# One decoder trunk on one core: four more weight chunks of the conditioning are summed during the first MLP, and the stage between the MLPs is issued in another order

## The chip, the cores and the metric

The kernel runs on one core of one Trainium2 chip. The metric is the device time of one execution in microseconds (us). TensorE (PE) multiplies, with its weight loads (PEld) beside it; VectorE (DVE), ScalarE (ACT) and GpSimd (POOL) do the rest; SyncE (SP) issues nearly all loads from HBM through one queue, in order. Engines wait for each other through semaphores.

## The reference

```python
for layer in range(2):                       # D_MODEL 1024, SEQ 256, BATCH 1, float32
    mod = (silu(c) @ ada_w[layer] + ada_b[layer])[:, None, :]
    sh_a, sc_a, gt_a, sh_m, sc_m, gt_m = jnp.split(mod, 6, axis=-1)
    h = modulate(rms_norm(x, attn_norm[layer]), sh_a, sc_a)
    mix = diff_attention(h, ...) if layer == 0 else nsa_attention(h, ..., *shared)
    x = x + gt_a * mix
    h = modulate(rms_norm(x, mlp_norm[layer]), sh_m, sc_m)
    x = x + gt_m * squared_relu_mlp(h, mlp_w1[layer], mlp_w2[layer])   # hidden width 4096
    if layer == 0:
        sh_kv, sc_kv = jnp.split(silu(c) @ kv_ada_w + kv_ada_b, 2, axis=-1)
        shared = nsa_shared_kv(modulate(rms_norm(x, kv_norm), sh_kv, sc_kv), ...)
return rms_norm(x, final_norm)
```

`modulate(h, shift, scale)` is `h * (1 + scale) + shift`. `nsa_attention` has 16 query heads that read one compressed and two full sets of keys and values.

## The kernel before

**Products.** Every weight is brought in as a chunk of 1 MB (`raw`), split by ACT into a rounded high part (`wh`, line 260) and by DVE into the remainder (`wl`, line 262), in two halves each, and multiplied in three products (lines 267 to 269; the rows of `rows_acc` and `proj_t` have these lines). Three chunks can wait as `raw` (pool `rawp`), three as `wh`/`wl` (pool `wp`). A load is issued when the chunk that held its buffer has been split.

**Adaptive weights.** The vectors `mod` come from 48 further chunks of 1 MB, twelve vectors of four chunks each, in a list: `gate(l, 2)` and `gate(l, 5)` are the two gates, `shift` and `scale` the others. A *tick* takes the next chunk and adds it on DVE, in two instructions, to `acc` (lines 416 and 418). After a vector's fourth tick PE turns it (line 447) and DVE finishes it (lines 455 to 458), or, for a gate, PE sums it (line 481) and DVE adds it to `gt` (line 482). Chunks of ticks come from two buffers, and during the first MLP from three more (`lend`).

**Stages.** Layer A's attention; MLP 0; a short stage with the residual (`ORDER_AB`); layer B (`ORDER_B`); MLP 1; the end. An MLP has 16 steps; in a step PE multiplies a chunk of w1 (`proj_t`) and one of w2 (`rows_acc`), ACT applies relu and square (lines 591 and 592), and `ticks[f]` says how many ticks step f has. The stages between are recorded in an order written out by hand as a list of names, each of which advances one generator by a step: `kc`, `vc`, `k1`, `k2`, `g`, `q0` to `q3` are projections, `p` the products of the compressed keys (line 1227), `h0` to `h7` the heads, `r0` to `r2` the output projection, `W` and `w` split steps, `a` a tick, `d` the end of a vector, `F` a load of `cmp_w1`, `x` filler products, `n0` and `n1` the residual and norm of either half of the rows, `y0` and `y1` the first products of MLP 1. `in_order` keeps that order on PE, ACT, DVE and SP.

**Compressed keys.** `kc` and `vc` are projections whose results are copied (`u`, line 1189; for `kc` on DVE, for `vc` on ACT) and rearranged by eight DMAs that POOL issues (`Z`, lines 1192 and 1193); DVE adds positions (`M`, line 1214, steps `m0` and `m1`), and `p` multiplies M with the `cmp_w1` chunks. Queries are scaled from PSUM by ACT (`qs`, line 1262) before the scores (line 1373) and the compressed scores (line 1327).

Of the kernel before, what the change touches and what calls it, by code (L numbers as in the profile page):

```python
# [44 lines left out]
n0 n1 n0 n1 w n0 n1 w v2 x v1 v2 v2 n1 n1 n1 n1 n1 v1 v2 F v1  # L45
"""
ORDER_B = """
kc kc W w W W w W vc a kc a w w W w vc W vc W a W w w k1 F k1 w m0 m1 p p W k1 a k2 W g W p p w W p k2 w g v1 p p p q0
k2 w W q0 w g W z q0 g g q1 h0 w g w W h0 z h0 h1 q1 h0 W h0 h0 q1 h0 h1 z c0 h0 c0 h2 h1 h0 c0 h1 c0 v2 d c0 h0 c0 h0
h2 h1 h2 h1 h0 h1 a h1 h1 h2 h3 h3 h3 q2 w h0 q2 h1 a h1 h3 q2 h2 h2 w h4 h2 W h2 h2 a h3 h2 W q3 w q3 h1 h3 h1 W h4 a  # L50
h2 h5 h3 h3 h3 h5 h4 h5 h4 q3 h5 h2 h3 W h4 w c1 h4 W c1 h3 h5 h4 c1 h6 h5 c1 d h4 d w h4 c1 r0 h4 c1 w h6 w h4 h3 h4
h5 h6 h2 h3 h7 W h5 h4 h6 h5 w h5 h7 r0 h7 r0 h7 h6 h6 h5 h7 r0 h6 h5 h6 r0 a r1 W h6 h7 a W h6 r1 h6 h6 r1 r1 w h5 h6
r1 a h7 h7 h7 w a h7 W h7 h7 h7 r2 w r2 d n0 W r2 n0 w n0 n0 n0 d r2 n0 n1 n0 n0 n1 r2 n1 n0 x n0 n1 x n0 n0 n1 n1 n0
W x n1 n1 y0 y0 n1 n1 n1 n1 w W n1 y0 x w y1 n1 n1 y0 y1 W y1 W w y1 w
"""
ORDER_END = """
r r r r r n0 n0 n0 n0 n0 n1 n1 n0 n1 n1 n1 n1 n1
# [621 lines left out]
def tall(w, i):  # L679
    return [P, 8, 256], [(lambda t: t, w[D * i : D * i + D, :].rearrange("(t p) c -> p t c", p=P))]  # L680
# [38 lines left out]
def trunk(net, scratch):  # L719
# [81 lines left out]
    def ada_steps(key, kind, w, col, finish):  # L801
        items.extend(rows(w[:, col : col + D], 256 * i) for i in range(4))
        net.steps.extend((kind, i, finish) for i in range(4))
# [4 lines left out]
    gate = lambda l, i: ada_steps((l, i), long, ada[l], D * i, net.ada_gate((l, i), ap["ada_b"][l : l + 1, D * i : D * i + D]))  # L808
# [7 lines left out]
    scale(("kv", 1), ap["kv_ada_w"], D, long, kvb[:, 8:16], kvn)  # L816
    shift((1, 0), ada[1], 0, long, adab(1, 0))
    scale((1, 1), ada[1], D, long, adab(1, 1), an(1))
    gate(1, 2)
    shift((1, 3), ada[1], 3 * D, long, adab(1, 3))  # L820
    scale((1, 4), ada[1], 4 * D, long, adab(1, 4), mn(1))
    gate(1, 5)
    weights.steps = weights.high_parts(), weights.low_parts()
    net.ada = Stream(net, net.adap, items, 2)
# [7 lines left out]
    with tc.tile_pool(name="attn_a", bufs=2) as net.work, ExitStack() as slices:  # L832
# [4 lines left out]
        hT = net.pair()  # L837
# [249 lines left out]
        def first_values():  # L1087
            plan.need("v7")
            for g in range(2):
                vv[g] = new("v")  # L1090
                for t in range(2):
                    nc.scalar.copy(vv[g][:, t, :], vs[t][:, g * 256 : g * 256 + 256])
                plan.mark(f"first{g}")
                yield

        def more_bias():
            plan.need("table")
            for g in range(4):
                if g > 1:
                    plan.need(f"scored{g - 2}")  # L1100
                biases[g] = load_bias(net.work, 4 * g, 4, 1)
                yield

        def rows_chunk(i):
            plan.need(f"heads{i}", *(f"rows{j}" for j in range(i)))
            if i == 0:
                acc.extend(net.accumulators())
            steps = weights.until_done(net.rows_acc(acc, [(weights.pop(f"r{i}"), oT, 2 * i)], i == 0, False), 5)
            yield from plan.finally_mark(steps, 5, f"rows{i}")

        def rows_end():
            plan.need("heads2", "heads3", "rows0", "rows1")
            parts = [(weights.pop("r2"), oT, 2 * i) for i in (2, 3)]
            yield from net.last_rows(net.rows_acc(acc, parts, False, True), plan, "sum")

        acc, early_ps, hT2 = [], {}, net.pair_late()
        weights.turns = deque("q2 k2 v2 q3 k3 v3 r0 r1 r2 r2 y0 y1".split())
        plan.work = dict(
            W=weights.steps[0], w=weights.steps[1], a=net.ticks(), d=net.endings(), L=weights.further(), x=net.busy(3), v=first_values(), b=more_bias(),
            r0=rows_chunk(0), r1=rows_chunk(1), r2=rows_end(),  # L1120
            n0=net.token_input(0, acc, lambda: net.mod[(0, 2)], [mods(0, 3)], hT2, plan, "sum"),
            n1=net.token_input(1, acc, lambda: net.mod[(0, 2)], [mods(0, 3)], hT2, plan, "sum"),
# [13 lines left out]
    nc.gpsimd.dma_start(w2c, ap["cmp_w2"].rearrange("s (k p) d -> p s k d", p=P))  # L1136
    spare = ExitStack()
    extra = spare.enter_context(tc.tile_pool(name="spare", bufs=3, side="right"))
    net.ada.lend(extra, 3, 20)
    talls = Stream(net, extra, [tall(ap["cmp_w1"][s], a) for a in range(2) for s in range(2)], 0)  # L1140

    def tall_loads():
# [3 lines left out]

    loads = tall_loads()
    with tc.tile_pool(name="mlp0", bufs=2) as net.work:
        acc, last = net.mlp(hT, early_ps, [0, 0, 4, 1, 1, 2, 1, 1, 2, 1, 1, 2, 2, 2, 0, 0])
        plan = Plan()  # L1150
        pairs = net.pair_late(2)
        given = acc, lambda: net.mod[(0, 5)], [mods("kv", 0), mods(1, 0)], pairs, plan, "sum"
        plan.work = dict(
            W=weights.steps[0], w=weights.steps[1], a=net.ticks(), d=net.endings(), L=weights.further(), F=loads, x=net.busy(3), r=net.last_rows(last, plan, "sum"),
            n0=net.token_input(0, *given), n1=net.token_input(1, *given),
        )
        kv_ps = {}
        weights.turns = deque(["v1", "v2"])
        plan.work.update({f"v{i}": net.early_proj_x(f"v{i}", pairs, plan, 0, kv_ps) for i in (1, 2)})
        plan.run(ORDER_AB)  # L1160
        hkv, hT = pairs

    with ExitStack() as st:
        pool = lambda name, bufs: st.enter_context(tc.tile_pool(name=name, bufs=bufs))
        keep = pool("attn_b1", 1)
        k1 = lambda name, shape: keep.tile(shape, F32, name=name)
# [19 lines left out]
        def for_blocks(s):  # L1186
            ps = yield from project("kv"[s] + "c")
            kvc = net.u([P, 2, T])
            (nc.scalar.copy if s else nc.vector.tensor_copy)(kvc, ps)
            for g in range(2):  # L1190
                src = kvc[g * 64 : g * 64 + 64]
                nc.gpsimd.dma_start(Zv[0:64, s, :, g, :], src)
                nc.gpsimd.dma_start(Zv[64:128, s, :, g, 0:255], src[:, :, 1:256])
            plan.mark(f"pairs{s}")
            yield

        def keys(br):
            ps = yield from project(f"k{br + 1}")
            nc.scalar.copy(kt[:, :, br, :], ps)
            plan.mark(f"keys{br}")  # L1200
            yield

        def values(br):
            nc.scalar.copy(vv[:, br], kv_ps[f"v{br + 1}"])
            plan.mark(f"values{br}")
            yield

        def blocks(s):
            plan.need(f"pairs{s}")
            for a in range(2):  # L1210
                src = Z[:, s].rearrange("p g (n t w) -> p t g n w", w=2, t=8)[:, :, :, a : a + 15, 0]
                dst = M[s][:, 8 * a : 8 * a + 8, 0:60].rearrange("p t (g n) -> p t g n", g=4)
                pb = pos[:, s, 8 * a : 8 * a + 8].unsqueeze(2).unsqueeze(3).broadcast_to([P, 8, 4, 15])
                nc.vector.tensor_add(dst, src, pb)
            plan.mark(f"blocks{s}")
            yield

        z = []
# [81 lines left out]
        def gating():  # L1300
            gps = yield from project("g", act=hT, cols=1, backward=True)
            graw = net.u([P, T])
            nc.scalar.copy(graw, gps[:, 0, :])
            yield
            ps = net.bank([P, 2, P])
            for qb in range(2):
                nc.tensor.transpose(ps[:, qb, :], graw[:, P - qb * P : T - qb * P], ident)
            yield
            nc.vector.tensor_scalar_max(gates, ps[:, :, 80:128], -80.0)
            yield  # L1310
            nc.scalar.activation(gates, gates, AF.Exp, scale=-1.0)
            yield
            nc.vector.tensor_scalar_add(gates, gates, 1.0)
            nc.vector.reciprocal(gates, gates)
            plan.mark("gates")
            yield
# [117 lines left out]
        def rows_end():  # L1434
# [5 lines left out]
        acc, early_ps, pairs, heads_out = [], {}, net.pair_late(), net.pair_late()  # L1440
# [3 lines left out]
            W=weights.steps[0], w=weights.steps[1], a=net.ticks(), d=net.endings(), L=weights.further(), F=loads, x=net.busy(3), kc=for_blocks(0), vc=for_blocks(1),  # L1444
            k1=keys(0), v1=values(0), k2=keys(1), v2=values(1), m0=blocks(0), m1=blocks(1),
            p=block_products(), z=hidden(), g=gating(), c0=compressed(0), c1=compressed(1),
            r0=rows_chunk(0), r1=rows_chunk(1), r2=rows_end(), n0=net.token_input(0, *given), n1=net.token_input(1, *given),
# [7 lines left out]
    with tc.tile_pool(name="mlp1", bufs=2) as net.work:  # L1455
        acc, last = net.mlp(hT, early_ps, [0, 0, 0, 1, 0, 1, 0, 1, 0, 1, 0, 0, 0, 0, 0, 0])
# [19 lines left out]
```

## Time and profile before

| what | us |
|---|---|
| median of 3 runs (716.26 to 718.22) | 716.46 |
| the profiled execution | 716.31 |
| its span, first to last instruction | 714.5 |
| PE busy in it | 676.0 (95%) |
| DVE busy | 533.0 (75%) |
| ACT busy | 390.0 (55%) |

The span is 1.8 us shorter than the execution's own time. In the span, MLP 0 runs from about 175 to 336 us, the residual stage to about 369, layer B to about 515 and MLP 1 from about 528 to 695. A busy share is an average over all stages; which engine the others wait for is read stage by stage.

### The profile page before, as it was taken

To read this page: it belongs to the slowest core of one execution; us is meant where nothing else is said; L and a number is where in the kernel's file an instruction comes from. 1 tells how busy PE (TensorE), PEld (TensorE's weight loads), DVE (VectorE), ACT (ScalarE), POOL (GpSimd) and SP (SyncE) were. 2 spreads that over 40 slices of the span, in tenths; PEclk is the share of its full clock that TensorE was granted. 3 is DMA by queue.
4 is the path that set the end of the run, shared out by engine and by line. 5 is a ranking of instruction groups with operands and counts; after the bars stand their busy time and mean duration, and the time that the engine had idled before them with its cause. 6 is when DMAs were issued, how large, how long until landed. Compare 5 with 4: busy or idle time off the path is not lost.

```text
span 714.5 us, 12065 instructions
## 1 busy us (share of the span) xinstructions
PE 676.0 (95%) x4719; PEld 594.7 (83%) x4719; DVE 533.0 (75%) x1012; ACT 390.0 (55%) x773; POOL 24.5 (3%) x46
## 2 busy tenths in 40 slices
PE   5699999999999999999897999989999999999995
PEld 4588998679889999998796786767799999989984
DVE  5686999888778787786897489889885465564545
ACT  3324976757256455454662268786574545444543
POOL 4010000000000000000002010000000000000000
PEclk9799999999999999999899899989999999999999
DMA  9999887896979888899569962963856557646411
GB/s 276 315 321 339 263 314 282 304 330 201 336 257 320 306 311 291 317 360 314 197 207 273 286 148 92 252 186 122 294 167 216 192 183 274 214 149 201 153 80 59
DMA packets 107272, 173.33 MB, mean 243 GB/s; under 512 B 3568, under 2 KB 78560, under 8 KB 107216
## 3 DMA queue, kind: packets, MB, share of 16 engines
q1 hardware_dynamic: 103840, 163.13, 69.3%
q0 software_dynamic: 2784, 8.38, 4.1%
q10 hardware_dynamic: 592, 1.05, 0.4%
q8 instruction: 37, 0.61, 0.4%
q14 instruction: 19, 0.16, 0.1%
HBM read 170.43 MB, written 1.07 MB: 240 GB/s over the span
## 4 chain that ended last, share of the span: by engine, by line
PE 78%; DMA 9%; DVE 6%; ACT 5%; issue 2%; SPq 0%; ACTq 0%; DVEq 0%
PE ps L267 21%; PE ps L269 20%; PE ps L268 20%; DMA ada_s<-ada_w 3%; DMA raw<-ada_w 2%; ACT e L660 2%; DMA raw<-b_w_out 2%; PE ps L281 2%; PE ps L286 2%; PE ps L282 2%; PE ps L1227 1%; DMA raw<-a_w_in 1%; DVE wl L262 1%; PE ps L1373 1%; PE ps L447 1%
## 5 line engine op out<-in xcount | busy, mean ns | idle before, releaser
L262 DVE TENSOR_TENSOR wl<-raw,wh 128x1024 fp32r<-128x1024 f32 x178 | 209.1, 1214 | 55.5 <-ACT wh L260 55.5
L260 ACT ACTIVATE wh<-raw 128x1024 fp32r<-128x1024 f32 (+1 forms) x178 | 179.1, 1047 | 111.8 <-DMA raw<-mlp_w 43.2
L267 PE MATMUL ps<-ah,wh 128*128 128x256 f32 x648 | 184.3, 284 | 0.0
L269 PE MATMUL ps<-ah,wl 128*128 128x256 f32 x648 | 183.2, 283 | 0.0
L268 PE MATMUL ps<-al,wh 128*128 128x256 f32 x648 | 183.1, 283 | 0.0
L267 PEld LDWEIGHTS ps<-ah,wh 128*128 128x128 f32 x648 | 123.9, 191 | 2.5 <-issue 2.2
L268 PEld LDWEIGHTS ps<-al,wh 128*128 128x128 f32 x648 | 123.9, 191 | 0.0
L269 PEld LDWEIGHTS ps<-ah,wl 128*128 128x128 f32 x648 | 123.8, 191 | 0.0
L267 PE MATMUL ps<-wh,uh 128*128 128x512 f32 (+1 forms) x320 | 113.0, 353 | 0.6 <-ACT uh L598 0.6
L269 PE MATMUL ps<-wh,ul 128*128 128x512 f32 (+1 forms) x320 | 112.1, 350 | 0.0
L268 PE MATMUL ps<-wl,uh 128*128 128x512 f32 (+1 forms) x320 | 111.6, 349 | 0.0
L418 DVE SCALAR_TENSOR_TENSOR acc<-raw,cact,acc 128x1024 f32<-128x1024 f32 x77 | 98.8, 1283 | 4.1 <-DMA raw<-ada_w 2.2
L599 DVE TENSOR_TENSOR ul<-uu,uh 128x512 fp32r<-128x512 f32 x28 | 19.3, 690 | 66.4 <-ACT uh L598 66.4
L267 PEld LDWEIGHTS ps<-wh,uh 128*128 128x128 f32 x320 | 60.3, 188 | 10.1 <-ACT uh L598 1.4
L269 PEld LDWEIGHTS ps<-wh,ul 128*128 128x128 f32 x320 | 60.1, 188 | 9.3 <-DVE ul L599 0.9
L268 PEld LDWEIGHTS ps<-wl,uh 128*128 128x128 f32 x320 | 60.3, 188 | 8.9 <-issue 0.5
L591 ACT ACTIVATE r<-ps 128x512 f32<-128x512 f32 x32 | 19.1, 597 | 86.0 <-PE ps L269 81.5
L660 ACT ACTIVATE e<-e,t 128x128 f32<-128x128 f32 (+1 forms) x96 | 42.4, 448 | 7.3 <-DVE t L655 7.2
L267 PE MATMUL ps<-wh,ah 128*128 128x512 f32 (+1 forms) x128 | 45.6, 357 | 0.0
L268 PE MATMUL ps<-wl,ah 128*128 128x512 f32 (+1 forms) x128 | 43.2, 338 | 0.0
L269 PE MATMUL ps<-wh,al 128*128 128x512 f32 (+1 forms) x128 | 43.2, 337 | 0.0
L655 DVE CUSTOM_DVE_ANT_0 e<-ps,bias 128x128 f32<-128x128 f32 (+1 forms) x96 | 28.3, 353 | 2.6 <-PE ps L667 1.7
(252 smaller groups left out, 965.9 us busy)
## 6 DMA issues: line engine op xcount, KB each, us to landing
raw<-mlp_w SPq DMA_DIRECT2D x64, 1024.0 KB, 8.1
raw<-ada_w SPq DMA_DIRECT2D x40, 1024.0 KB, 6.5
ada_s<-ada_w SPq DMA_DIRECT2D x16, 512.0 KB, 7.8
raw<-kv_ada_w SPq DMA_DIRECT2D x8, 1024.0 KB, 7.8
w_s<-a_w_in SPq DMA_DIRECT2D x8, 768.0 KB, 7.6
raw<-a_w_in SPq DMA_DIRECT2D x6, 1024.0 KB, 5.6
raw<-w_kv SPq DMA_DIRECT2D x6, 1024.0 KB, 7.1
raw<-b_w_in SPq DMA_DIRECT2D x9, 512.0 KB, 9.0
```

The source lines that it names most:

```text
L260: nc.scalar.activation(to(h), of, AF.Copy)
L262: nc.vector.tensor_sub(to(l), of, to(h).bitcast(F32))
L267: mm(out, lh, rh, start=first, stop=False, **kw)
L268: mm(out, lh, rl, start=False, stop=False, **kw)
L269: mm(out, ll, rh, start=False, stop=last, **kw)
L281: mm(ps[:, t, :], hh[:, k, c], wh[:, k, :], start=k == 0, stop=False)
L282: mm(ps[:, t, :], hh[:, k, c], wl[:, k, :], start=False, stop=False)
L418: nc.vector.scalar_tensor_tensor(acc, raw[:, j, :], cc, acc, op0=ALU.mult, op1=ALU.add)
L591: nc.scalar.activation(r, ps, AF.Relu)
L599: nc.vector.tensor_sub(ul, u, uh.bitcast(F32))
L655: self.nc.vector.tensor_tensor_reduce(out=out, in0=s, in1=bias[:, T - n : T], scale=-1.0, scalar=BIG, op0=ALU.add, op1=ALU.min, accum_out=neg)
L660: self.nc.scalar.activation(part, part, AF.Exp, bias=neg, scale=-1.0, accum_out=total)
```

## The change

The list of vectors gets another order at one place: the gate of layer B's attention, `gate(1, 2)`, moves behind the shift and scale of layer B's MLP. MLP 0 has 24 ticks where it had 20, two in each step from 2 to 13, and `ORDER_B` has 8 where it had 12; MLP 1 keeps its 4. The chunks that MLP 0 sums in addition are those of `shift((1, 3))`. `ORDER_B` is a new arrangement of the same steps, less four `a` and two `d`. The arithmetic stays as it was.

```diff
 ORDER_B = """
-kc kc W w W W w W vc a kc a w w W w vc W vc W a W w w k1 F k1 w m0 m1 p p W k1 a k2 W g W p p w W p k2 w g v1 p p p q0
...
+W kc W W kc W w v1 W w vc W kc a vc w w a k1 k1 vc m0 w W w W W k2 m1 w F w a p p W a w k2 g W W p p k2 w k1 g p g d W
...
     scale((1, 1), ada[1], D, long, adab(1, 1), an(1))
-    gate(1, 2)
     shift((1, 3), ada[1], 3 * D, long, adab(1, 3))
     scale((1, 4), ada[1], 4 * D, long, adab(1, 4), mn(1))
+    gate(1, 2)
     gate(1, 5)
...
-    net.ada.lend(extra, 3, 20)
+    net.ada.lend(extra, 3, 24)
...
-        acc, last = net.mlp(hT, early_ps, [0, 0, 4, 1, 1, 2, 1, 1, 2, 1, 1, 2, 2, 2, 0, 0])
+        acc, last = net.mlp(hT, early_ps, [0, 0, 2, 2, 2, 2, 2, 2, 2, 2, 2, 2, 2, 2, 0, 0])
```

**Place 1, DVE at the start of layer B.** Twelve rows up to M0 before, ten up to M1 now. `u ... <-ps` is the copy of `kc`'s result; raw_..._3914 before and raw_..._3945 after is the chunk of `k1`, 4090 and 4096 that of `k2`, 4096 and 4128 that of `g`. Before:

```order
L262 TENSOR_TENSOR wl_593_4093<-raw_582_3914,wh_592_4092 128x1024
L416 TENSOR_SCALAR acc_597_4126<-raw_508_3449,cact_122 128x1024
L418 SCALAR_TENSOR_TENSOR acc_597_4126<-raw_508_3449,cact_122,acc_597_4126 128x1024
L1189 COPY u_599_4131<-ps_588_4036 128x512
L418 SCALAR_TENSOR_TENSOR acc_597_4126<-raw_509_3453,cact_122,acc_597_4126 128x1024 x2
L262 TENSOR_TENSOR wl_593_4093<-raw_582_3914,wh_592_4092 128x1024
L262 TENSOR_TENSOR wl_602_4144<-raw_591_4090,wh_601_4143 128x1024
L418 SCALAR_TENSOR_TENSOR acc_597_4126<-raw_598_4129,cact_122,acc_597_4126 128x1024 x2
L262 TENSOR_TENSOR wl_606_4182<-raw_594_4096,wh_605_4181 128x512
L262 TENSOR_TENSOR wl_602_4144<-raw_591_4090,wh_601_4143 128x1024
L262 TENSOR_TENSOR wl_606_4182<-raw_594_4096,wh_605_4181 128x512
L1214 TENSOR_TENSOR M0_4028<-Z_4027,colB_134 128x8x60 x2
```

Now:

```order
L262 TENSOR_TENSOR wl_604_4131<-raw_599_4096,wh_603_4130 128x1024
L1189 COPY u_607_4163<-ps_598_4070 128x512
L416 TENSOR_SCALAR acc_608_4169<-raw_516_3481,cact_122 128x1024
L418 SCALAR_TENSOR_TENSOR acc_608_4169<-raw_516_3481,cact_122,acc_608_4169 128x1024
L262 TENSOR_TENSOR wl_601_4099<-raw_590_3945,wh_600_4098 128x1024
L418 SCALAR_TENSOR_TENSOR acc_608_4169<-raw_517_3485,cact_122,acc_608_4169 128x1024 x2
L1214 TENSOR_TENSOR M0_4059<-Z_4058,colB_134 128x8x60 x2
L262 TENSOR_TENSOR wl_604_4131<-raw_599_4096,wh_603_4130 128x1024
L262 TENSOR_TENSOR wl_614_4263<-raw_602_4128,wh_613_4262 128x512
L1214 TENSOR_TENSOR M1_4060<-Z_4058,colB_134 128x8x60 x2
```

The copy of `kc` now stands behind the first half of `k2`'s split, the tick of a third chunk is gone from ahead of M0, and the second half of `k2`'s split stands behind M0 instead of ahead of it.

**Place 2, PE around the products of the compressed keys.** ps_609 before and ps_611 after are `k1`, ps_615 and ps_618 `k2`. Before, the last row of `k1` and what follows:

```order
L269 MATMUL ps_609_4194<-ah_559_3807,wl_593_4093 128x256
L1227 MATMUL ps_611_4250<-raw_538_3684,M0_4028 64x256
L1227 MATMUL ps_611_4250<-raw_575_3866,M1_4029 64x256
L1227 MATMUL ps_611_4250<-raw_538_3684,M0_4028 64x256
L1227 MATMUL ps_611_4250<-raw_575_3866,M1_4029 64x256
```

Now, the last rows of the first half of `k2` and what follows:

```order
L268 MATMUL ps_618_4273<-al_568_3839,wh_603_4130 128x256
L269 MATMUL ps_618_4273<-ah_567_3838,wl_604_4131 128x256
L1227 MATMUL ps_622_4311<-raw_546_3715,M0_4059 64x256
L1227 MATMUL ps_622_4311<-raw_583_3897,M1_4060 64x256
L1227 MATMUL ps_622_4311<-raw_546_3715,M0_4059 64x256
```

Between `k1` and `p` there now stand 24 products of `k2`, which before came behind the first 16 of `p`.

**Place 3, SP from the last projections to the output projection.** `b_w_in` are chunks of queries, `b_w_out` those of the output projection, `ada_w` those of ticks. Before:

```order
L245 DMA raw_617_4326<-b_w_in 128x8x128 x2
L245 DMA raw_622_4378<-b_w_in 128x8x128 x2
L245 DMA raw_627_4447<-b_w_out 64x2x1024 x2
L245 DMA raw_695_4749<-ada_w 128x2x1024
L245 DMA raw_714_4852<-ada_w 128x2x1024
L245 DMA raw_720_4891<-b_w_out 64x2x1024 x2
```

Now:

```order
L245 DMA raw_620_4304<-b_w_in 128x8x128 x2
L245 DMA raw_621_4309<-ada_w 128x2x1024
L245 DMA raw_623_4331<-ada_w 128x2x1024
L245 DMA raw_627_4405<-b_w_in 128x8x128 x2
L245 DMA raw_645_4520<-b_w_out 64x2x1024 x2
L245 DMA raw_654_4555<-b_w_out 64x2x1024 x2
```

No load of a tick's chunk stands between the loads of `b_w_out` any more.

## Rows read from the trace of the kernel before

**Rows 1.** Busy time by stage: stretch, its us, each engine, PEclk, DMA share, GB/s

```profile
175.00:336.00 161.00, 161.00 (x1104) 148.91 (x1103) 128.08 (x127) 78.86 (x95) 0.00 (x0) 1.00 0.88 313
374.00:420.00 46.00, 40.99 (x320) 36.37 (x319) 29.24 (x37) 13.40 (x21) 7.49 (x12) 0.93 0.92 255
420.00:460.00 40.00, 39.00 (x294) 29.56 (x294) 38.54 (x140) 30.79 (x99) 2.89 (x4) 1.00 0.63 163
460.00:480.00 20.00, 17.65 (x108) 12.45 (x108) 17.31 (x67) 16.68 (x56) 0.72 (x1) 0.83 0.71 169
```

**Rows 2.** Timeline of PE at 389 and at 466 us: start, us, what, idle before

```profile
388.95 0.62 PE L1227 MATMUL ps<-raw,M 128*64 128x256 f32 x2 [2.23 <-DMA raw<-ada_w]
392.34 1.55 PE L1227 MATMUL ps<-raw,M 128*64 128x256 f32 x6 [2.77 <-issue]
...
466.15 1.07 PE L1327 MATMUL ps<-kcz,qs 128*128 128x32 f32 x4 [2.05 <-ACT qs L1262]
```

**Rows 3.** Busy time in 2 us, with columns as in group 1

```profile
392.00:394.00 2.00, 1.66 (x8) 1.14 (x10) 2.00 (x3) 0.40 (x1) 0.00 (x0) 0.50 1.01 384
```

**Rows 4.** Chain that ended last, pieces from several stretches: start, us, what

```profile
195.23 1.72 PE ps L481 x4
231.02 0.87 PE ps L447 x8
...
392.34 6.13 PE ps L1227 x30
...
399.25 0.12 PE ps L269
...
404.37 3.60 PE ps L1227 x32
...
446.56 11.71 DMA raw<-b_w_out
...
465.62 0.49 ACT qs L1262
```

**Rows 5.** Timeline of DVE at the start of layer B

```profile
375.24 0.69 DVE L1189 COPY u<-ps 128x512 f32<-128x512 f32 x1
...
387.79 1.82 DVE L1214 TENSOR_TENSOR M<-Z,colB 128x480 f32<-128x480 f32 x2
391.27 1.85 DVE L1214 TENSOR_TENSOR M<-Z,colB 128x480 f32<-128x480 f32 x2 [1.67 <-DMA Z<-u]
```

**Rows 6.** Instructions and DMAs of the tile Z: ns min/median/max; landing

```profile
L1192 POOL DMA_DIRECT2D Z<-u x4: 598/600/632, 376.2 to 383.1; - x4
...
DMA to landing us min/median/max: 6.7/6.9/7.5
```

**Rows 7.** Timeline of ACT in layer B

```profile
375.12 2.01 ACT L260 ACTIVATE wh<-raw 128x1024 fp32r<-128x1024 f32 x2 [2.70 <-PE ps L268]
...
458.35 1.06 ACT L260 ACTIVATE wh<-raw 128x1024 fp32r<-128x1024 f32 x1 [3.02 <-DMA raw<-b_w_out]
```

**Rows 8.** Timeline of SP's queue in layer B

```profile
414.15 1.30 SPq L245 DMA_DIRECT2D raw<-b_w_out  x2
440.35 5.45 SPq L245 DMA_DIRECT2D raw<-ada_w  x2
```

**Rows 9.** Timeline of ACT in two steps of MLP 0

```profile
313.16 0.60 ACT L591 ACTIVATE r<-ps 128x512 f32<-128x512 f32 x1 [2.04 <-PE ps L269]
...
324.51 0.60 ACT L591 ACTIVATE r<-ps 128x512 f32<-128x512 f32 x1 [2.92 <-PE ps L269]
```

**Rows 10.** Timeline of DVE in a step of MLP 0 with two ticks

```profile
315.73 5.24 DVE L418 SCALAR_TENSOR_TENSOR acc<-raw,cact,acc 128x1024 f32<-128x1024 f32 x4
320.89 4.63 DVE L262 TENSOR_TENSOR wl<-raw,wh 128x1024 fp32r<-128x1024 f32 x4
```

**Rows 11.** Busy time in 5 us of MLP 0, with columns as in group 1

```profile
298.00:303.00 5.00, 5.00 (x39) 4.74 (x39) 5.00 (x6) 1.86 (x3) 0.00 (x0) 1.00 0.99 381
...
318.00:323.00 5.00, 5.00 (x45) 5.00 (x44) 4.93 (x5) 2.44 (x3) 0.00 (x0) 1.00 1.03 414
```

More of the change, by code (lines that the diff above doesn't have):

```diff
@@ L47 @@
 ORDER_B = """
-kc kc W w W W w W vc a kc a w w W w vc W vc W a W w w k1 F k1 w m0 m1 p p W k1 a k2 W g W p p w W p k2 w g v1 p p p q0
[L49 to L54, printed above, removed]
+W kc W W kc W w v1 W w vc W kc a vc w w a k1 k1 vc m0 w W w W W k2 m1 w F w a p p W a w k2 g W W p p k2 w k1 g p g d W
+w q0 g p p v2 q0 W g p q0 d h0 w g w z h0 W h0 w h1 z q1 h0 q1 q1 W w c0 h0 h1 h0 h0 h2 h0 w h1 c0 c0 h1 c0 q2 z W c0
+h0 c0 h0 h3 h2 h1 h0 h1 h1 h2 h1 h2 h1 h3 q2 h3 h1 h2 h2 h0 h3 h1 h1 h2 W h2 q2 h0 h2 h2 h3 h3 q3 h1 W h4 w h2 h4 W h4
+h3 q3 h4 h2 h3 q3 h5 h3 c1 w h4 h4 h2 h3 h5 h5 W h3 c1 c1 h5 h4 h6 c1 h3 h4 c1 w h5 h4 c1 h4 r0 h6 h4 W h4 h5 w h4 w
+h5 r0 h6 h3 w h5 h5 h7 h5 h6 h7 h6 h5 h6 h7 r0 h7 r0 r0 h5 a h6 h6 r1 h7 h6 r1 W h6 r1 h6 h7 h7 a h5 h6 h6 h7 r1 h7 h7
+w h7 a W r1 h7 w h7 W w a r2 W w r2 d r2 n0 n0 n0 r2 n0 n1 n0 n0 n1 r2 W n0 x n1 n0 n0 n0 n1 x n0 x n0 n1 n1 n0 y0 y0
+n1 x W n1 n1 n1 W n1 w n1 y0 n1 w n1 n1 y1 y0 W y1 w y1 y1 w
 """
```

## The prediction

> **What bounds the kernel now.** I read the busy times by stage first. In MLP 0 PE is busy for all of its 161.00 us at the full clock; nothing that the change adds there can shorten it, and whatever it adds must stay hidden behind PE. In layer B PE is not always busy: 40.99 of 46 us from 374, 39.00 of 40 us from 420, 17.65 of 20 us from 460, and in the first and third of these stretches the granted clock is 0.93 and 0.83 instead of 1.00 [rows 1]. So what there is to win lies in layer B. PE's timeline shows where: it stands 2.23 and 2.77 us ahead of the first products of the compressed keys at 389 us, and 2.05 us at 466 us [rows 2]. Behind the first of these the clock is at its lower level, 0.50 [rows 3], that is 1.2 GHz. The lower clock costs 46 x 0.07 = 3.2 us and 20 x 0.17 = 3.4 us of PE's time in the two stretches [rows 1]; another view of the same is that 30 products of line 1227 took 6.13 us at 392 us and 32 of them 3.60 us at 404 us [rows 4], which is 2.75 us more for the like amount.
>
> What is late in the two places is read next. At 389 and 392 us it is M: DVE begins M0 at 387.79 us and M1 at 391.27 us, the latter after a wait for the DMAs into Z [rows 5]. At 466 us it is the scaled queries: the chain that ended last goes from a `b_w_out` load of 11.71 us over ACT to the copy `qs` at 465.62 us [rows 4]; ACT waited 3.02 us for that load with exponentials and the copy queued behind it [rows 7]. The load was late because SP, after 414.15 us, issued nothing until 440.35 us, when a tick's chunk could go [rows 8]; the `b_w_out` loads stood behind it.
>
> **MLP 0: four more ticks, cost 0 taken.** Four loads of 1 MB (1.049 million bytes) and eight DVE additions move here. DVE: a step with two ticks holds four additions in 5.24 us and four splits in 4.63 us [rows 10] and one `ul` (0.7 us at most); together 10.6 us against a step of 324.51 - 313.16 = 11.35 us [rows 9]. The two splits that the next `rows_acc` needs end at about 320.89 + 2.3 = 323.2 us, 1.2 us before PE comes to them at about 324.4 us [rows 9, 10]. Every second step also turns a vector, which lengthens PE's step by 0.87 us [rows 4]. The 2-tick steps of the kernel before ran without a PE wait [rows 1], and the new list makes all twelve like them, so DVE fits. DMA: a step moves four chunks, 4.19 million bytes, in a mean of 11.35 + 0.43 = 11.78 us, which is 356 GB/s. MLP 0 as a whole moves 313 x 161 = 50.4 million bytes, and with four chunks more 54.6, or 339 GB/s [rows 1]. What the engines can do: 313 / 0.88 = 356 GB/s if they were always busy [rows 1], and 381 and 414 GB/s in stretches of 5 us in which they were [rows 11]. So the loads fit too, but with little to spare; I take 0, with a bound of 7.5 us, worked out under the rivals. Less than 0 is excluded, since PE has no idle time there.
>
> **Start of layer B: -2.9 us.** The new order puts half of `k2`, 24 products at 0.12 us [rows 4] or 2.88 us, between `k1` and `p`. I follow the two queues from the end of `kc` at 375.12 us, when ACT gets its buffer [rows 7]. ACT splits `k2`'s first half (1.0 us), DVE follows (1.2 us), and only then copies `kc`: it ends at 378.1 us instead of 375.24 + 0.69 = 375.9 us [rows 5]. Four DMA issues of 0.60 us and a landing of 6.9 us [rows 6] put Z at about 387.1 us, so M0 (1.82 us [rows 5]) ends near 389.0 us, as before, though a tick is gone from ahead of it. The second half of `k2`'s split now stands behind M0 and ends near 390.1 us. PE has done `k1` at 386.7 us and the part of `k2` that needs the first half at 388.1 us; it waits 2.0 us and ends `k2`'s half at about 391.6 us. M1 hangs on `vc`, whose place on PE has not moved, so its first half is done at 391.27 + 0.93 = 392.2 us [rows 5]. `p` therefore starts where it did, 392.2 us against 392.34 us, with 2.88 us of work done ahead. I keep the lower clock behind it, since a wait of 2.0 us remains and one of 2.05 us was followed by it at 466 us [rows 1, 2]. If the clock stays up, 2.75 us more are won; if M1's DMAs land 2.9 us later beside the weight loads that now run ahead of the ticks' chunks, nothing is won.
>
> **Middle of layer B: -5.5 us, less 1.0 us.** No tick's load stands among the `b_w_out` loads any more, and four ticks of DVE (4 x 2.62 = 10.5 us by [rows 10]) have left the stage, which from 420 us has DVE busy for 38.54 of 40 us [rows 1]. So the 26 us in which SP issued nothing go, ACT's 3.02 us go, and with them the 2.05 us of PE and the 3.4 us of lower clock behind them: 5.45 us. What is late next: now the scores of head 0 stand directly behind `q0` on PE, and the compressed scores behind `q1`; each must wait for the copy `qs`, 0.49 us [rows 4], where other products lay between. That gives back 2 x 0.5 = 1.0 us. Bounds: 0 if ACT, which still has the same exponentials, makes PE wait at another copy; -6.8 us if the 1.0 us of other PE waits from 420 us [rows 1] go as well.
>
> **End of layer B: +1.2 us.** The gate comes last, so its sum stands between parts of the output projection: line 481 in place of line 447, 1.72 - 0.87 = 0.85 us [rows 4], which is a move and no addition over the kernel. But DVE can begin the residual only when the gate is complete; I work out 1.4 us later for the norm of the first rows, of which the 0.85 us are covered by PE. That leaves 0.6 us, and a split half (a quarter of 4.63 us, 1.2 us [rows 10]) now stands ahead of the second rows' norm, half of it hidden by filler: 0.6 us. Bounds 0 and 4.6 us (1.2 us and a lower clock of 3.4 us behind a longer wait).
>
> **Sum.** 0 - 2.9 - 5.5 + 1.0 + 1.2 = -6.2 us on the profiled execution's 716.31 us (span 714.5 us and 1.8 us around it): 710.1 us. The median of the runs, 716.46 us, is 0.15 us above that execution, so the same difference from it gives 710.3 us. I say 710.2 us.
>
> **Rivals.** *MLP 0 starves.* Speaking for it: the loads need 356 GB/s for eleven steps, and the engines' mean while busy was 356 GB/s [rows 1], with no margin. Against it: 381 and 414 GB/s in busy stretches [rows 11], and the new list spreads what the old one loaded in a burst of four ticks. It decides from about 345 GB/s downward: a step then takes 12.15 us, 0.37 us too long, and eleven of them are 4.1 us, about all the slack that a late load has (DVE takes up the splits only at 320.89 us, behind 5.2 us of additions [rows 10], and ACT needs 1 us before it); beyond that PE waits, some 4 us in all if the rate is lower still, with 3.4 us of lower clock behind it [rows 1]. With the gains in layer B that is 710.2 + 7.5 = 717.7 us, slower than before. The Trainium skill, "DMA: Bandwidth & Descriptors", section "Where 436 GB/s comes from", puts loads from HBM at about 358 GB/s; by that a step needs 11.71 us and the margin is 0.07 us, so the page speaks for this rival. The 414 GB/s of a 5 us stretch [rows 11] is above the page's figure, and by the row the step fits.
>
> *Both falls of the clock go.* For it: the wait at 388 us is 2.0 us where 5.0 us were [rows 2]. Against it: the 2.05 us at 466 us. It gives 710.2 - 2.75 = 707.5 us, and 706.2 us with the 1.3 us less of other waits.
>
> *The new order only moves the waits.* For it: M1 still hangs on the same DMAs, and ACT's and PE's work in layer B is the same, so the copies `qs`, or a split of ACT that waits for a `q2` load ahead of its copies, may stop PE for 2 us somewhere else, with a lower clock behind it. Against it: the load that is named as late no longer stands behind a tick. If the middle's 5.5 us come back as another wait and fall, and the start gives 2.9 us: 715.7 us, which a measurement can't tell from no change.
>
> **How the numbers follow.** Forecast 0.44; both falls gone 0.24; waits only moved 0.18; MLP 0 starves 0.14. A measurement of this kernel can tell about 0.3%, 2.1 us, from no change. The first two are faster, 0.68, and of the third a fifth, 0.03; of the third the rest is same, 0.13, and a little slower, 0.02; the fourth is slower for the most part, 0.12, and same for 0.02. So faster 0.71, same 0.15, slower 0.14. The range takes in the second case's lowest value with 2 us for an unknown wait that goes, 704 us, and reaches up to 717 us, half of the fourth case. The forecast's own range is 708 to 713 us.
>
> **What would show it.** Right: PE 100% busy in MLP 0 with DMA near 340 GB/s; PE's wait ahead of line 1227 short, with `k2` in the middle of it; no ACT wait for `b_w_out`, and no lower clock around 460 us. Wrong: a PE wait in the last steps of MLP 0 with ACT waiting for `mlp_w`; a lower clock at a new place in layer B, behind a copy `qs` or a split that waits for `b_w_in`; a wait of PE at line 375 for the late gate.

## Result, and the profile after

The changed kernel takes 705.53 us (median of 4 runs, 704.99 to 707.99) against 716.36 us in the runs beside it: a ratio of 0.986 with a 95% interval of 0.982 to 0.989. It is faster by 10.8 us; 710.2 us was forecast, with a range of 704 to 717 us. A second set of five runs of it gave 706.40 us and 0.9855 (0.9828 to 0.9881). The profiled execution took 705.53 us, 10.78 us less than the one of before, and its span is 703.8 us.

The busy times by stage of the changed kernel, in the stretches and columns of [rows 1]:

```profile
175.00:336.00 161.00, 161.00 (x1104) 148.87 (x1103) 139.43 (x138) 79.81 (x96) 0.00 (x0) 1.00 0.95 338
374.00:420.00 46.00, 42.58 (x335) 36.51 (x334) 33.70 (x51) 15.39 (x26) 7.49 (x12) 0.96 0.91 268
420.00:460.00 40.00, 39.68 (x323) 32.49 (x321) 33.83 (x152) 36.13 (x122) 3.62 (x5) 1.00 0.55 119
460.00:480.00 20.00, 20.00 (x147) 13.95 (x144) 18.51 (x78) 19.04 (x65) 0.00 (x0) 1.00 0.26 70
```

MLP 0 has 11 us more of DVE and 25 GB/s more of loads under a PE that is as busy as before. In layer B PE is busier in all three stretches, and from 460 us the clock is whole and the DMA engines are busy for 0.26 of the time instead of 0.71.

PE and DVE at the start of layer B, the places of [rows 2] and [rows 5]:

```profile
389.80 0.65 PE L1227 MATMUL ps<-raw,M 128*64 128x256 f32 x2
393.18 5.22 PE L1227 MATMUL ps<-raw,M 128*64 128x256 f32 x30 [2.73 <-issue]
```

```profile
383.86 1.91 DVE L1214 TENSOR_TENSOR M<-Z,colB 128x480 f32<-128x480 f32 x2
385.68 1.82 DVE L262 TENSOR_TENSOR wl<-raw,wh 128x1024 fp32r<-128x1024 f32 x2
392.09 1.87 DVE L1214 TENSOR_TENSOR M<-Z,colB 128x480 f32<-128x480 f32 x2 [4.59 <-DMA Z<-u]
```

M0 is done long before it is needed; only M1 still holds PE, for 2.73 us instead of 2.23 and 2.77 us. The waits of PE that the view lists from there to the output projection (line waited for: us, times, longest):

```profile
PE ps L1373 <- ACT qs L1262: 0.7, 1, 0.7
PE ps L1327 <- ACT qs L1262: 0.3, 1, 0.3
```

ACT's waits for DVE's pieces of the softmax from 420 to 460 us, before and after:

```profile
ACT e L660 <- DVE t L655: 2.8, 3, 1.4
ACT e L1393 <- DVE t L1389: 1.4, 3, 0.7
```

```profile
ACT e L660 <- DVE t L655: 0.8, 3, 0.4
```

SP's queue in layer B: the `b_w_out` loads follow each other, as [rows 8] did not:

```profile
398.01 0.37 SPq L245 DMA_DIRECT2D raw<-cmp_w  x1
...
416.52 39.29 SPq L245 DMA_DIRECT2D raw<-b_w_out  x8
```

Where the time went, by the start of one and the same instruction in both traces (third and last relu of MLP 0; filler products in the residual stage; the second 32 products of line 1227; the last sum or turn ahead of the residual, L447 at 508.40 us before and L481 at 496.15 us after; first relu of MLP 1):

| stretch | before | after | difference | of it, work that only moved | rest |
|---|---|---|---|---|---|
| up to MLP 0 | 178.30 | 178.90 | +0.60 | | +0.6 |
| MLP 0 | 158.45 | 159.35 | +0.90 | +0.87 (a turn) | 0.0 |
| residual stage | 24.51 | 23.28 | -1.23 | | -1.2 |
| start of layer B | 43.04 | 42.71 | -0.33 | +2.88 (24 products of `k2`) | -3.2 |
| middle | 104.10 | 91.91 | -12.19 | -2.88 and -1.72 (a sum) | -7.6 |
| end of layer B | 20.37 | 21.87 | +1.50 | +0.85 (sum for turn) | +0.65 |

The differences add up to -10.75 us; MLP 1 takes 165.33 us in both. Each row stands on one trace of either kernel, and two stretches that the change does not touch moved too: over all the runs below, which leave the code ahead of MLP 0 as it is, the first row lies between 178.15 and 180.24 us, and the residual stage takes 23.3 to 24.5 us. So the middle is where most was won, and the question for the runs was why: by the loads of `b_w_out`, as I had worked it out, by DVE's additions, or by the new order alone.

### The profile page after: what moved, and what is told of

The parts are those of the page before. It is cut to its first block, busy times and chain, and to the rows that moved or that the text cites. A ratio compares the mean times of both kernels' runs of the same rounds, so it can differ in the third digit from the quotient of the medians.

```text
span 703.8 us, 12063 instructions
## 1 busy us (share of the span) xinstructions
PE 668.6 (95%) x4719; PEld 589.8 (84%) x4719; DVE 533.0 (76%) x1012; ACT 388.8 (55%) x773; POOL 24.5 (3%) x46
## 4 chain that ended last, share of the span: by engine, by line
PE 85%; DMA 5%; DVE 4%; ACT 3%; issue 1%; SPq 0%; ACTq 0%; DVEq 0%
PE ps L267 22%; PE ps L269 22%; PE ps L268 22%; DMA ada_s<-ada_w 3%; PE ps L281 2%; PE ps L1373 2%; PE ps L282 2%; PE ps L286 2%; DMA raw<-a_w_in 1%; PE ps L1227 1%; PE ps L447 1%; PE ps L1414 1%; PE ps L481 1%; DVE wl L262 1%; ACT wh L260 1%
## 5 line engine op out<-in xcount | busy, mean ns | idle before, releaser
L262 DVE TENSOR_TENSOR wl<-raw,wh 128x1024 fp32r<-128x1024 f32 (+1 forms) x178 | 209.2, 1214 | 42.6 <-ACT wh L260 42.5
L267 PEld LDWEIGHTS ps<-wh,uh 128*128 128x128 f32 x320 | 60.3, 188 | 10.1 <-ACT uh L598 1.4
```

The source lines that it names most:

```text
L262: nc.vector.tensor_sub(to(l), of, to(h).bitcast(F32))
L267: mm(out, lh, rh, start=first, stop=False, **kw)
```

## The experiments

Line numbers of the kernels below are one higher than those of before and after, thirteen in layer B of the one with dummy additions.

**The middle: order and ticks apart.** First the old order with the new ticks:

```diff
-... v2 d c0 ... h1 h0 h1 a h1 h1 ... h0 q2 h1 a h1 h3 ... h2 h2 a h3 h2 ... W h4 a h2 ... c1 d h4 d w ... d r2 n0
+... v2 d c0 ... h1 h0 h1 h1 h1 ... h0 q2 h1 h1 h3 ... h2 h2 h3 h2 ... W h4 h2 ... c1 d h4 w ... r2 n0
```

> The order of layer B of the kernel before, with the new list of vectors and 24 ticks in MLP 0; the four ticks of the middle and two ends of vectors are taken out of the order, the rest of it stays. Theory A (loads): the gain in the middle of layer B, 7.7 us by the two traces, comes from the four chunks of ticks no longer standing in SP's queue among the loads of b_w_out. Then this kernel keeps it, loses the 2.9 us of the start, and takes 716.4 - 7.7 + 1.2 (the late gate) = 709.9 us, 709 to 711; ACT has no wait for b_w_out and no lower clock follows the copies qs. Theory B (arrangement): the gain comes from what stands ahead of what on PE and ACT; then PE still waits about 2 us for a copy qs with a lower clock behind it, and the time is 714 to 717 us.

It took 722.43 us, ratio 1.0086 (1.0054 to 1.0117): slower than before, outside both theories. The `b_w_out` loads were in time, and still ACT came to the copy `qs` as late as before: 61.5 us behind the start of the second 32 products of line 1227, against 61.2 us in the kernel before. Another wait, for PE, had taken the place of the late load. ACT's timeline:

```profile
462.48 0.86 ACT L1404 COPY pT<-ps 128x384 f32<-128x384 f32 x2 [3.84 <-PE ps L668]
...
467.08 0.57 ACT L1263 ACTIVATE qs<-ps 128x512 f32<-128x512 f32 x1
```

The lower clock came too (0.83 from 460 to 480 us). At the end of layer B it took 24.65 us from the gate's sum to MLP 1, 4.3 us more than before; 1.7 us of this are a fall of the clock (0.66 from 520 to 525 us). Taking the ticks out of the old order gains nothing.

Next the new order with the old ticks:

```diff
-    net.ada.lend(extra, 3, 24)
+    net.ada.lend(extra, 3, 20)
-        acc, last = net.mlp(hT, early_ps, [0, 0, 2, 2, 2, 2, 2, 2, 2, 2, 2, 2, 2, 2, 0, 0])
+        acc, last = net.mlp(hT, early_ps, [0, 0, 4, 1, 1, 2, 1, 1, 2, 1, 1, 2, 2, 2, 0, 0])
-... h0 h1 h1 h2 ... h2 h2 h0 h3 ... h2 h2 h3 h3 ... W h4 h3 ... r0 h6 h4 W h4
+... h0 h1 a h1 h2 ... h2 h2 a h0 h3 ... h2 h2 a h3 h3 ... W h4 a h3 ... r0 d h6 h4 W d h4
```

> The new order of layer B with four ticks (and two ends of vectors) put back into its middle, about where the kernel before had them, and MLP 0 with its 20 ticks as before. Theory A (loads): ACT waits about 3 us for a late b_w_out chunk again, PE about 2 us for what stands behind it on ACT, and a lower clock follows: 705.5 + 5.5 to 7.7 = 711 to 713 us; the start of layer B is as in the changed kernel. Theory B (arrangement): the late loads are hidden in the new order, 705 to 707 us.

713.80 us, ratio 0.9958 (0.9937 to 0.9980), near what theory A said. But the chain of waits names something else than a load. Its pieces from 444 us on:

```profile
444.36 1.21 DVE acc L419
...
449.19 1.20 DVE acc L419
450.42 1.28 DVE acc L419
...
455.53 1.14 DVE wl L263
456.67 1.21 DVE acc L419
...
457.90 1.28 DVE acc L419
459.19 0.20 DVE e L656
459.43 0.66 ACT e L661 x3
...
462.08 0.51 ACT qs L1263
...
462.63 1.41 PE ps L1328 x11
```

The additions of a tick stand between the pieces of the softmax on DVE; ACT's exponentials and behind them the copy `qs` come later by as much. That gave a third theory and two runs, the loads without the additions and the additions without the loads:

```diff
+    scale((1, 4), ada[1], 4 * D, lambda i, raw, end: net.ada_long(i, raw, end, 64), adab(1, 4), mn(1))
-    scale((1, 4), ada[1], 4 * D, long, adab(1, 4), mn(1))
+                nc.vector.scalar_tensor_tensor(acc[:, :n], raw[:, j, :n], cc, acc[:, :n], op0=ALU.mult, op1=ALU.add)
-                nc.vector.scalar_tensor_tensor(acc, raw[:, j, :], cc, acc, op0=ALU.mult, op1=ALU.add)
```

> As e2_new_order_old_ticks, with seven of the eight additions of the four ticks in the middle of layer B done on 64 of 1024 columns (this leaves most of one vector out of the result); their loads and their places in SP's queue stay. Theory A (loads): the loads among those of b_w_out make the difference of 6.0 us between that kernel and the changed one, so the time stays at 712 to 714 us. Theory C (DVE): it is the additions, 2.6 us for a tick, that stand between the pieces of the softmax on DVE; then the time is 706 to 708 us, and the copies qs come as early as in the changed kernel.

706.90 us, ratio 0.9863 (0.9837 to 0.9890), as theory C said. SP's queue again held tick loads among those of `b_w_out`, and PE did not notice; SP's timeline, and PE's waits from 374 to 505 us:

```profile
437.08 8.07 SPq L246 DMA_DIRECT2D raw<-ada_w  x3
445.25 1.49 SPq L246 DMA_DIRECT2D raw<-b_w_out  x2
```

```profile
PE ps L1228 <- issue: 2.4, 1, 2.4
PE ps L1374 <- ACT qs L1263: 0.7, 1, 0.7
PE ps L376 <- ACT xn L539: 0.6, 1, 0.6
PE ps L1328 <- ACT qs L1263: 0.3, 1, 0.3
```

```diff
-... h0 h1 h1 h2 ... h2 h2 h0 h3 ... h2 h2 h3 h3 ... W h4 h3 ...
+... h0 h1 E h1 h2 ... h2 h2 E h0 h3 ... h2 h2 E h3 h3 ... W h4 E h3 ...
+        acc = self.accp.tile([P, D], F32, tag="acc", name=self.name("acc"))
...
+                    nc.vector.scalar_tensor_tensor(acc, raw, cc, acc, op0=ALU.mult, op1=ALU.add)
```

> The changed kernel, with eight additions of 1024 columns on DVE (into a buffer that nothing reads, from data that lie there) at the four places in the middle of layer B where e2_new_order_old_ticks has its ticks; no load, no turn of a vector. Theory C (what matters in the new order is DVE's additions): 705.5 + 6.0 = 711.5 us, 710.5 to 713. Theory D (additions matter only together with the loads, whose landing they wait for): 705.5 to 708 us.

713.88 us, ratio 0.9959 (0.9936 to 0.9981): 7.5 us above the changed kernel on the same chip, without one load more, and 0.9 us above the range of theory C. PE again waits for what ACT does behind DVE, and the lower clock is back (0.83 from 460 to 480 us). PE's timeline:

```profile
462.86 0.63 PE L1340 MATMUL ps<-kcz,qs 128*128 128x32 f32 x4 [1.07 <-ACT pT L1416]
463.73 2.77 PE L1340 MATMUL ps<-kcz,qs 128*128 128x32 f32 x12 [0.24 <-ACT qs L1275]
```

Side by side, the middle of layer B (as in the table above, from second 32 products of line 1227 to last sum or turn), made alike by taking off the `k2` products (2.88 us), a sum (1.72 us) or a second turn (0.87 us) where a kernel has them in this stretch:

| order | additions there | loads there | stretch, us | made alike |
|---|---|---|---|---|
| old (before) | yes | yes | 104.10 | 99.5 |
| old | no | no | 104.56 | 101.7 |
| new | yes | yes | 98.80 | 97.9 |
| new | yes (dummies) | no | 99.48 | 99.5 |
| new | 1 of 8 whole | yes | 92.89 | 92.0 |
| new (after) | no | no | 91.91 | 91.9 |

By these traces, one for each row, the new order alone is worth 1.6 us, the ticks' leaving alone costs 2.2 us, both together give 7.6 us. The 1.6 us are no more than a shorter fall of the clock: from 460 to 480 us it is 0.91 in the new order with the ticks and 0.83 before, which is 20 x 0.08 = 1.6 us. The new order with the ticks:

```profile
460.00:480.00 20.00, 18.69 (x126) 12.74 (x124) 18.50 (x73) 17.96 (x58) 0.72 (x1) 0.91 0.59 148
```

So it isn't shown that the new order alone gains anything in the middle. In the new order the loads cost 0.1 us and the additions 5.9 to 7.6 us, by the same difference of clock. The delay behind them is the same with and without the loads: counted from the second 32 products, the fourth copy `qs` begins at 51.9 us in the changed kernel, at 52.0 us with the loads alone, and at 57.6 us both with the dummies and with the whole ticks.

**The start: the wait on M1.** Two kernels were to fill it, one with work, one with fillers:

```diff
-... W k2 m1 w F w a p p W a w k2 g W W p p k2 ...
+... W k2 m1 w F w a p k2 p W a w g W W p p k2 ...
```

> The second half of k2 (24 products, 2.9 us of PE) moved ahead of the first products of the compressed keys, where the changed kernel waits 2.7 us with 3.4 us of lower clock behind it. Theory A (this wait hangs on M1 alone, and the clock falls because of the wait): the wait is filled, the fall goes, and the time is 705.5 - 2.7 - 1.7 = 701.1 us, 700 to 702. Theory B (the fall comes whatever fills the wait, or what k2 covered between the later products turns into a wait for the split of g): 703 to 706 us.

```diff
-... W k2 m1 w F w a p p W a w k2 g ...
+... W k2 m1 w F w a p x x x x x x x p W a w k2 g ...
```

> Seven filler steps, 21 products of 256 columns that nothing reads, put ahead of the first products of the compressed keys, where PE waits 2.7 us in the changed kernel. They should take 2.3 to 3.1 us. Theory A (the clock falls there because PE stands still): no lower clock behind the wait, which is worth 1.7 us by the trace (3.4 us at half speed): 703.8 us. Theory B (the clock falls there for another reason, or what was lost at the lower clock comes back as a wait for the fourth cmp_w chunk, as in e4_second_k2_ahead): 705 to 706 us.

They took 710.37 us (0.9912, 0.9891 to 0.9933) and 710.69 us (0.9910, 0.9889 to 0.9932), 4 to 5 us slower than the changed kernel and outside what either theory said, by an edit of mine that missed its place: there are two `p` in a row, and the work stood between them, behind the wait and not in it. What it delayed is instructive. The fourth `cmp_w` chunk can be issued only when the first 32 products have freed its buffer. With `k2` between the two `p`, SP issued it at 401.94 us in place of 398.01 us, and PE stood for it:

```profile
407.53 5.35 PE L1228 MATMUL ps<-raw,M 128*64 128x256 f32 x30 [2.00 <-DMA raw<-cmp_w]
```

The same two with the work ahead of both `p`:

```diff
-... W k2 m1 w F w a p p W a w k2 g W W p p k2 ...
+... W k2 m1 w F w a k2 p p W a w g W W p p k2 ...
```

> In e4_second_k2_ahead the 24 products of k2 stood behind the first sixteen products of the compressed keys, not ahead of them. Here they stand ahead of all of these. The wait of 2.7 us on M1 is then filled with 2.9 us of work and no lower clock should follow, so the first 32 products end at 396.8 us. But the fourth cmp_w chunk is issued only when they are done, and landed 5.6 us later in the changed kernel: 402.4 us, while between them and the second 32 products only the 2.9 us of g are left. Theory A (the wait hangs on M1 and the clock on the wait): the second 32 products begin at 402.4 us in place of 404.2 us, 703.7 us, with up to 1.7 us of that lost again if a lower clock follows the wait of 2.7 us for cmp_w. Theory B (M1 comes later in step, or the clock falls anyway): 705 us or more.

```diff
-... W k2 m1 w F w a p p W a w k2 g ...
+... W k2 m1 w F w a x x x x x x x p p W a w k2 g ...
```

> As e8_fillers_ahead_of_p, where the fillers too stood behind the first sixteen products; here the 21 filler products stand ahead of all products of the compressed keys. Theory A (the clock falls because PE stands still there): the wait is filled, the first 32 products take 3.6 us at the full clock, and all that follows comes 1.6 us sooner, the fourth cmp_w chunk too: 703.9 us. Theory B (the fillers take longer than the wait, or the clock falls anyway): 705 to 707 us.

The one with `k2` took 707.29 us (0.9867, 0.9841 to 0.9893), the one with fillers 705.92 us (0.9849, 0.9821 to 0.9877); the changed kernel beside them took 706.40 us:

> The changed kernel unaltered, beside the other three of this call on one chip, so that differences of 1 to 2 us can be read against it: 705.5 us, 704.5 to 707, and a ratio to the kernel before of 0.985.

In both the wait on M1 was filled and no lower clock followed, as theory A has it, but the times are those of theory B. PE with the fillers, and the clock of the stretch (1.00, where [rows 1] has 0.93):

```profile
390.33 2.47 PE L568 MATMUL ps<-ones 128*128 128x256 bf16 x21
392.73 0.65 PE L1228 MATMUL ps<-raw,M 128*64 128x256 f32 x2
393.60 3.64 PE L1228 MATMUL ps<-raw,M 128*64 128x256 f32 x30 [0.23 <-issue]
403.07 0.65 PE L1228 MATMUL ps<-raw,M 128*64 128x256 f32 x2
404.39 3.67 PE L1228 MATMUL ps<-raw,M 128*64 128x256 f32 x30 [0.68 <-DMA raw<-cmp_w]
```

```profile
374.00:420.00 46.00, 44.41 (x359) 38.48 (x358) 34.17 (x51) 15.16 (x26) 7.51 (x12) 1.00 0.92 267
```

The 1.7 us that the clock gave were gone 10 us later: the fourth `cmp_w` chunk was issued at 396.87 us, 1.4 us sooner than in the changed kernel's second set, but took 7.5 us to land in place of 5.6, and the second 32 products began in earnest at 404.39 us, against 404.50 us in the changed kernel's second set. With `k2` moved, less work is left ahead of that landing, and the wait and the lower clock reappear there:

```profile
403.33 6.31 PE L1228 MATMUL ps<-raw,M 128*64 128x256 f32 x30 [3.42 <-DMA raw<-cmp_w]
```

**MLP 0: when it starves.** Four ticks more again, first as threes:

```diff
-        acc, last = net.mlp(hT, early_ps, [0, 0, 2, 2, 2, 2, 2, 2, 2, 2, 2, 2, 2, 2, 0, 0])
+        acc, last = net.mlp(hT, early_ps, [0, 0, 2, 3, 2, 2, 3, 2, 2, 3, 2, 2, 3, 2, 0, 0])
-    net.ada.lend(extra, 3, 24)
+    net.ada.lend(extra, 3, 28)
-... vc W kc a vc w w a k1 k1 ... F w a p p W a w k2 g ... g d W w ... q0 d h0
+... vc W kc vc w w k1 k1 ... F w p p W w k2 g ... g W w ... q0 h0
```

> 28 ticks in MLP 0, three in every third step; layer B keeps only the four of the gate. MLP 0 then has to load 58.8 million bytes in 161 us, 365 GB/s. If the engines keep the 381 to 414 GB/s of their busy stretches, PE stays busy in MLP 0 and the time is 704 to 706 us (the wait ahead of the products of the compressed keys hangs on Z, not on the ticks). If about 356 GB/s, the mean while they were busy, is the limit, MLP 0 takes 165 us at least, with lower clocks behind its waits: 709 to 714 us. DVE, with 139 + 10.5 us of work in 161 us, should not be the bound but for single steps of 13.2 us.

732.34 us, ratio 1.0207 (1.0182 to 1.0232), worse than either guess. DVE's timeline shows a wait of which I had not thought:

```profile
210.11 0.75 DVE L417 TENSOR_SCALAR acc<-raw,cact 128x1024 f32<-128x1024 f32 x1 [5.25 <-PE ps L482]
...
239.03 0.75 DVE L417 TENSOR_SCALAR acc<-raw,cact 128x1024 f32<-128x1024 f32 x1 [7.05 <-PE ps L448]
```

There is one buffer `acc`. A step in which one vector ends and the next begins makes DVE wait for PE's sum or turn, with the splits that PE needs queued behind the waiting addition. Two ticks in each step never do that. So once more with whole vectors, four ticks in two steps:

```diff
-        acc, last = net.mlp(hT, early_ps, [0, 0, 2, 3, 2, 2, 3, 2, 2, 3, 2, 2, 3, 2, 0, 0])
+        acc, last = net.mlp(hT, early_ps, [0, 0, 4, 2, 2, 2, 2, 2, 2, 4, 2, 2, 2, 2, 0, 0])
```

> 28 ticks in MLP 0 again, but with no step in which a vector ends and the next begins: four ticks in two steps, two in the others. In e3_28_ticks_in_mlp0 DVE stood waiting for PE's turn of the vector before, 20.4 us in three waits. Theory A (that wait was the cause): MLP 0 is at most a few us longer than its 161 us, and the time is 704 to 710 us. Theory B (365 GB/s or the additions of a vector in one step are too much): PE waits for splits in the steps with four ticks, 5 us and more in each, with lower clocks behind: 715 us and more.

710.18 us, ratio 0.9906 (0.9879 to 0.9932), just above theory A. From third to last relu MLP 0 took 165.54 us, 6.2 us more than with 24 ticks, 0.87 us of it a turn that only moved. Most of the rest was lost at the late step with four. SP issued the vector's last chunk at 273.56 us, as DVE's addition of an earlier one ended; it took 6.86 us to land, DVE's last additions waited for it, and PE, which had to turn that vector next, waited for them. It is PE's only long wait in MLP 0, and a lower clock followed. Pieces of the chain that ended last, PE's waits from 179 to 350 us, and the busy times of MLP 0 and of that step:

```profile
272.25 1.30 DVE acc L419
273.56 6.86 DMA raw<-ada_w
280.51 1.30 DVE acc L419
281.83 1.30 DVE acc L419
...
283.27 1.06 PE ps L448 x8
```

```profile
PE ps L448 <- DVE acc L419: 2.7, 1, 2.7
PE ps L269 <- DVE wl L263: 0.2, 1, 0.2
```

```profile
175.00:336.00 161.00, 158.10 (x1066) 144.60 (x1065) 146.02 (x146) 74.95 (x92) 0.00 (x0) 0.99 0.98 351
...
280.00:299.00 19.00, 16.28 (x100) 14.30 (x99) 17.43 (x19) 6.27 (x8) 0.00 (x0) 0.91 0.97 335
```

The weight chunks came late as well, behind four tick chunks in SP's queue: ACT waited 11.20 us for one, until 293.70 us. But PE did not stand for it.

**The end: the late gate.**

```diff
     shift((1, 3), ada[1], 3 * D, long, adab(1, 3))
+    gate(1, 2)
     scale((1, 4), ada[1], 4 * D, long, adab(1, 4), mn(1))
-    gate(1, 2)
     gate(1, 5)
```

In the order one of the early `d` goes and a `d` comes behind the last `r2`.

> The list of vectors as the kernel before had it (the gate ahead of the shift and scale of the MLP is moved to stand between them), so that the four early ticks of layer B sum the gate and the four late ones the scale; PE's turn and DVE's end of the scale stand where the kernel before had them. Theory A (the late gate holds the residual up): from the last output projection to the first relu it takes 20.4 us again in place of 21.9 us, of which 0.85 us is only work that moves to an earlier place: the time is 705.5 - 0.7 = 704.8 us, 704 to 705.5. Theory B (the end of layer B hangs on something else): 705.5 us or more, and the stretch stays at 21.9 us less the moved 0.85.

706.08 us, ratio 0.9856 (0.9829 to 0.9882), as the changed kernel. From the last turn (496.91 us) to the first relu (518.03 us) it took 21.12 us, and 21.87 - 0.85 = 21.02 us were to be expected if the place of the gate cost nothing. Theory B holds.

## Why the prediction was right, and where it was not

Sign and range were right, and so was the place: layer B, with MLP 0 as cover. The time came out 4.7 us lower than forecast, below the forecast's own range of 708 to 713 us. Step by step:

- **MLP 0, 0: right.** PE was busy for 161.00 of 161 us, and the loads ran at 338 GB/s where 339 was worked out. The rival *MLP 0 starves* fell, but not by much: with four more ticks MLP 0 took 6.2 us longer, 0.87 us of it moved work, though PE stood there for a tick's chunk and not, as that rival has it, for weights. The Trainium skill, "DMA: Bandwidth & Descriptors", section "Where 436 GB/s comes from", has about 358 GB/s as one core's limit for loads from HBM; the 351 GB/s of that run, with the DMA engines at 0.98, agree with it as a mean over a stage, and the 414 GB/s of 5 us [rows 11] do not.
- **Start, -2.9: right in size (-3.2), wrong in details.** PE did not wait for `k2`'s split, since Z landed sooner than after 6.9 us (2.3 us at the least, below): M0 began at 383.86 us, without a wait. And M1 was 0.8 us later than worked out. The lower clock that was kept in the sum lasted from 392.9 to 396.3 us, half as long as before; what a whole clock would bring there turned out to be 0.1 us, because the next thing late is the fourth `cmp_w` chunk. So the 2.75 us of the rival *both falls of the clock go* were not to be had at this place; that the time lies near this rival's 706.2 us has another reason, the next step.
- **Middle, -5.5 + 1.0: the gain was mis-sized (-7.6), and the step to its cause failed.** The step read: SP's 26 us go, ACT's 3.02 us go, and with them PE's wait and the lower clock. The wait for `b_w_out` was in the trace of before, and it did end last there. But with it gone in the old order another wait stood in its place, and with the loads back in the new order nothing was lost. What the ticks cost in the new order are the 10.5 us of additions on DVE, which the prediction had named as a relief and not as the cause. The old order was not run with the loads alone or the additions alone, so that there, too, it was the additions is not shown. A sign of it before the change is [rows 1], DVE busy for 38.54 of 40 us, together with ACT's waits for DVE in that stage, shown with the profile after. The Trainium skill, "PSUM — Partial Sum Buffer", section "Engine vs sequencer instructions", says that the queues of ScalarE and VectorE are strict first in, first out; by that an addition of 1.2 us holds back every softmax piece behind it, and the trace with dummies agrees (7.6 us for eight additions). The two copies `qs` cost the 1.0 us that was put down for them, 0.7 and 0.3.
- **End, +1.2: smaller (+0.65), and not by the gate.** With the gate back in the middle nothing was won. In the old order, though, the late gate went with 24.65 - 0.85 - 20.37 = 3.4 us more, half of it by the fall of the clock named above. What the 0.65 us hang on was not tried; the split half ahead of the second norm, half of the term, is still a candidate.
- **The rival *the new order only moves the waits*** is what the old order did when its ticks were taken out.

Not foreseen are the 1.2 us of the residual stage: its lower clock lasted 3.4 us in place of 6.8 us. That is no effect of the change but luck of the two traces. The run with the dummies and the first one with fillers have MLP 0 and this stage as the changed kernel has them, and their clock was as low as before (0.91 from 336 to 374 us, and 24.4 and 24.3 us); the new order with the old ticks had 0.96 and 23.3 us, like the changed kernel. Without this row and the +0.6 us ahead of MLP 0 the gain is 10.1 us, still 3.9 us more than forecast, most of it in the middle. Open is which places of the old order hold it back once the ticks are gone.

## What to carry to other kernels

A load that ends a chain last is the cause only as long as nothing else stands just behind it: run the kernel with the load and without the work that comes with it, and the reverse, before putting a gain down to a queue. An order written out by hand fits the work for which it was written; work that leaves it and a new order have to be tried together: here, in the middle of layer B, neither alone gained anything clear of a fall of the clock (-1.6 and +2.2 us) and both gave -7.6 us. Before filling a wait ask what is late next: here the filled wait gave back 1.7 us of clock and 0.1 us of time.

## What the runs showed that I had not expected

The clock can fall without one long wait of PE. In the old order with the new ticks PE was busy for 0.71, 0.99, 0.66, 1.00 and 0.79 us in the five us from 462 us, its longest wait there was 0.34 us, and from 466.7 us the granted clock was 0.50 for 6.8 us. In the same order with the ticks, a wait of 2.05 us preceded the like fall.

How long a DMA takes to land varied by more than I had allowed. The Z DMAs, for which I took 6.9 us [rows 6], in the changed kernel (issues, and times to landing):

```profile
L1192 POOL DMA_DIRECT2D Z<-u x4: 598/600/632, 378.6 to 383.3; - x4
...
DMA to landing us min/median/max: 2.3/4.4/8.0
```

A spread from 6.7 to 7.5 us became one from 2.3 to 8.0 us for the same transfers. They now start 2.4 us later than before, and those of `kc`, the first four, were in by the time DVE came to M0. What made the difference was not tried; the loads in flight beside them are a candidate, since the two kernels issue different loads there.
